# Down product of a SwiGLU layer: row tiles loaded through GpSimd's queue, and the first chunk's operands begun with the last unit's sixth product

## The chip, the cores and the metric

The kernel runs on one core of one Trainium2 chip. The metric is the device time of one execution in microseconds. Three runs of the kernel before took 2215.3 us in the median (2212.56 to 2217.59).

## What is computed

Two layers over 1024 positions of 1024 features, all in float32. Each layer is a mixer and a SwiGLU layer, each with a residual sum; the mixer of the first layer is a short gated convolution, that of the second a dilated attention. The part that matters here is SwiGLU, with 2816 hidden features:

```python
def swiglu(h, w_gate, w_up, w_down):
    return (jax.nn.silu(h @ w_gate) * (h @ w_up)) @ w_down

def reference(x, ...):
    for i in range(DEPTH):            # DEPTH = 2
        ...
        h = rms_norm(x, ffn_norm[i])
        x = x + swiglu(h, w_gate[i], w_up[i], w_down[i])
    return rms_norm(x, final_norm)
```

## The kernel before, in words

Activations lie with features on the partitions and positions along the row: `X[n]` is a tile of 128 features by 1024 positions, a "page". Half a page is 128 x 512. Pages come from a pool of 41, half pages from a pool of 20.

**Exact products from rounded parts.** TensorE is given rounded numbers, so each operand is split into a hi and a lo part: ACT copies it with rounding (hi), VectorE subtracts (lo = value - hi). A product is then three matmuls: hi hi, hi lo, lo hi. For weights this is `split` (lines 137 and 138), for activations `Strassen.hi` (lines 497 and 498).

**Strassen-Winograd.** The large products are done as products of 2 x 2 blocks with seven multiplications instead of eight, numbered m = 1 to 7 and done in the order `WINOGRAD` = 1, 2, 6, 5, 7, 3, 4. The operands of m are the sums of blocks that the method asks for. The seven share banks of PSUM: p takes m = 1, 6, 7 and 4 one on top of the other, q takes m = 2, r takes m = 5 and 3. Between two of them the bank is read (line 515 adds it to a part, line 511 copies it, line 726 adds it to x), and the next product accumulates on what is there.

**Gate and up.** `products` (line 533) runs through 22 units, the even ones gate, the odd ones up, in an order written out by hand (`unit_order`). From unit 4 on, the products m = 2 and 4 of an odd unit and of the even one before it are divided a second time (`deeper`, line 586): products (u, 11) to (u, 17), of 256 columns, written here as (21, 11) and so on. The order ends:

```python
(20,6) (20,5) (20,7) (21,1) (20,3) (21,6) (21,5) (21,7)
(21,11) (21,12) (21,15) (21,16) (21,3) (21,17) (21,13) (21,14)
```

A take of weights (line 166) also issues the splits of the weights that come one to four products later. When a block of a hidden row is done, `out` (line 1108) multiplies it by the gate (line 1114) and `store` (line 660) writes it to device memory through GpSimd's queue: rows of pairs 0 to 8 as the seven operands of the down product (`self.parts[q, m]`, lines 668 and 687), rows 18 to 21 as they are (`self.plain`, line 664).

**Down.** The down product takes the 9 pairs in three chunks of 3 (c = 0, 3, 6), each in two calls of `down` (line 720), for the output tiles 0 to 3 and 4 to 7. For each m it does two products of 9 matmuls and adds each bank to two tiles of x (line 726). Its operands come from `feed` (line 694), a generator. Each step of it loads three tiles ("hin", half pages) of the next m from `self.parts`, then splits the three tiles of the m loaded by the step before: three copies on ACT (line 497) and three subtractions on VectorE (line 498). Eight steps make one chunk: seven load, the second to the eighth split.

**What sets the order.** The schedule is manual: each engine runs its instructions in the order in which the program issues them, and waits for what an instruction needs. The function `filled` (line 756) is called after each product of the list, and there the first chunk's feed is stepped (line 770): once after each product of unit 21 from (21, 16) on, five steps. The other three steps are taken in `down(0, 0)`, one after each m. The feeds of chunks 3 and 6 are stepped in the calls of `down` before theirs.

**Queues.** All raw weights (line 151), the tiles of x (line 692), the tiles of feed (line 702) and the plain rows (line 716) are loaded through SP's queue, in the order of the program. GpSimd's queue carries the stores of `store` here.

Of the kernel before, what the change touches and what calls it, by code (L numbers as in the profile page):

```python
# [30 lines left out]
DEEP, DEEPER = (2, 4), 10  # L31
# [10 lines left out]
CONV = "conv"  # L42
# [52 lines left out]
def trunk(ctx: ExitStack, tc: tile.TileContext, x, gains_in, cwi, ck, cwo, wqkv, wo, relb,  # L95
          wg, wu, wd, oneh, ident, out):
    nc = tc.nc
# [11 lines left out]
    def half_page(name, dt=F32):  # L109
        return scope["pool"].tile([128, 512], dt, name=name, tag="half", bufs=scope["halves"])  # L110
# [47 lines left out]
    def ensure(upto):  # L158
        while op_state[0] < min(upto + 1, len(ops)):
            key = ops[op_state[0] + 1][0] if op_state[0] + 1 < len(ops) else None  # L160
            if key in sums_of:
                sums_of.pop(key)()
            made[op_state[0]] = ops[op_state[0]][1]()
            op_state[0] += 1
# [49 lines left out]
    def add_deep(unit, key, u, rows, upto):  # L214
# [27 lines left out]
        def early(op):  # L242
            w = op()
            run(*[sums_of(j, m) for j, m in enumerate(DEEP)])
            return w
# [105 lines left out]
    def run(*gens):  # L351
        for _ in zip(*gens):
            pass
        for g in gens:
            for _ in g:
                pass
# [6 lines left out]
    def both(w, ks, acts):  # L363
        banks = two_banks()
        run(product(w, ks, acts, banks))
        return banks
# [106 lines left out]
    class Strassen:  # L473
# [220 lines left out]
        def feed(self, c):  # L694

            tiles = None
            for m in WINOGRAD + (None,):
                new = None
                if m:
                    new = [half_page("hin") for k in range(self.chunk)]  # L700
                    for k in range(self.chunk):
                        nc.sync.dma_start(new[k], self.parts[c + k, m])
                if tiles:
                    lows = [self.hi(last, k, t, nc.vector)
                            for k, t in enumerate(tiles)]
                    for lo in lows:
                        lo()
                tiles, last = new, m
                if m:
                    self.b[m] = [None] * self.chunk  # L710
                    yield
# [8 lines left out]
        def down(self, c, n, feed):  # L720

            p, r = {}, {}
            later = {2: (1,), 6: (3,), 5: (4,), 7: (6,), 3: (5,), 4: (7,)}

            def add(n, h, b):
                nc.vector.tensor_tensor(out=X[n][:, half(h)], in0=X[n][:, half(h)], in1=b, op=ALU.add)  # L726

            for m in WINOGRAD:
                for k in (n, n + 2):
                    if m == 1:  # L730
                        p[k] = bank()
                    if m == 5:
                        r[k] = bank()
                    b = bank() if m == 2 else r[k] if m in (3, 5) else p[k]
                    self.mm((c, k), m, b, m in (1, 2, 5), 4)
                    add(k + (m in (5, 7, 4)), int(m in (6, 5, 7, 3)), b)
                next(feed, None)
                if c == n == 0:
                    self.load_x(*later.get(m, ()))
                    self.rest(m)  # L740
# [10 lines left out]
        def run(self, start, hooks={}):  # L751

            self.base = op_state[1]
            last = self.nu - 1

            def filled(n):
                start(n)
                if self.key != CONV:
                    self.now = n + 1
                    i = self.order.index((3, 4))  # L760
                    if n == i - 15:
                        prep.append(self.deepen(2))
                    if n == i - 5:
                        prep.append(self.deepen(4))
                    for p in prep:
                        next(p, None)
                if self.key == CONV:
                    self.below(n, last)
                else:
                    if self.order[n][0] == last and n >= self.at(last, DEEPER + 6) - self.base:  # L770
                        next(feed, None)
                    if self.order[n] == (last, DEEPER + 7):
                        self.load_x(0, 2)
                        ensure(self.at(last, DEEPER + 4) + 4)
                self.idle(n)

            prep = []
            if self.key == CONV:
                self.products(filled, hooks)
                self.first_tiles()  # L780
                return
            feed = self.feed(0)
            self.products(filled, hooks)
            for c in range(0, self.pairs, self.chunk):
                self.down(c, 0, feed)
                feed = self.feed(c + self.chunk) if c + self.chunk < self.pairs else self.feed_last()
                self.down(c, 4, feed)
            run(feed)


    class Conv(Strassen):
# [148 lines left out]
        def first_tiles(self):  # L940

            run(self.low)
            upper = self.halved(range(CO, KT))
            for n in range(KT):
                banks = two_banks()
                run(product(take(("co", 0, n), 2), range(CO), self.hid, banks))
                if n + 2 < KT:
                    self.load_x(n + 2)
                add_to_x(n, banks)
                self.step(4 if n < 2 else None)  # L950
                if n >= 3:
                    next(upper, None)
            run(upper)
            for f in range(CO):
                del self.plain[f]
# [843 lines left out]
```

## Time and profile before

| | |
|---|---|
| median of three runs | 2215.3 us |
| the profiled execution | 2215.37 us |
| its span, first to last instruction | 2213.6 us |
| TensorE clock granted, mean | 0.985 |
| ACT busy | 998.4 us, 45% |
| GpSimd busy | 147.9 us, 7% |
| DMA through SP's queue (q1), share of 16 engines | 184.80 MB, 26.2% |
| DMA through GpSimd's queue (q0) | 45.46 MB, 5.6% |
| loads of feed (line 702) | 126, of 256 KB each |
| DMA over the span | 114 GB/s |

The page gives the busy time of each engine and groups of instructions by line. The waits say which engine stood idle, in front of which line, and what ended the wait; the one named is the one that came last by the profile, which need not be the one that was needed. The timeline shows instructions in order of time: start, duration, engine, line, operation, output and input; "x3" is three of the same in a row, and brackets hold the idle time of the engine before it and what ended it. PE is TensorE, DVE VectorE, ACT ScalarE, POOL GpSimd; SPq is the queue of SP.

The two SwiGLU layers behave alike. The stretches around their down products lie at about 740 to 940 us and 1960 to 2150 us of the span.

### The profile page before, as it was taken

The numbers are of one execution on the slowest core, as the hardware profiler recorded it, in microseconds if no ns is written. First come the engines' busy times: TensorE is split into PE (matmuls) and PEld (weight loads), VectorE is DVE, ScalarE is ACT, GpSimd is POOL, SyncE is SP. The second block draws the span as 40 slices with busy tenths as digits, with TensorE's granted clock in tenths as the row PEclk, the third lists the DMA queues.
The fourth block names the chain that finished last, engine by engine and source line by source line (L and its number), as shares of the span: only waits on it lengthen the run. The fifth ranks groups of instructions, "written<-read, shape, count | busy, mean of one in ns | idle before, by whom it ended". The sixth has DMA issues, their size and how long they took to land.

```text
span 2213.6 us, 30526 instructions
## 1 busy us (share of the span) xinstructions
PE 2143.2 (97%) x11138; PEld 1829.8 (83%) x11138; DVE 1769.8 (80%) x3255; ACT 998.4 (45%) x1808; POOL 147.9 (7%) x196
## 2 busy tenths in 40 slices
PE   7899999899999999999999999999899999999998
PEld 5788887688888878878999999887678888878887
DVE  7797758888888798965677767868988888889886
ACT  6433425444444444434455555534534444444435
POOL 0000000010101000010111111110010101000000
PEclk9999999999999999999999999999999999999999
DMA  4122541222323374423333333544113323266432
GB/s 154 53 84 74 208 131 51 86 98 90 117 93 114 106 269 153 131 86 131 90 90 91 90 90 83 168 130 140 62 72 102 113 96 119 96 218 210 155 93 77
DMA packets 131263, 255.30 MB, mean 115 GB/s; under 512 B 47386, under 2 KB 58666, under 8 KB 131114
## 3 DMA queue, kind: packets, MB, share of 16 engines
q1 hardware_dynamic: 75978, 184.80, 26.2%
q0 software_dynamic: 13968, 45.46, 5.6%
q10 hardware_dynamic: 41168, 23.10, 3.6%
q8 instruction: 88, 1.44, 0.3%
q14 instruction: 61, 0.50, 0.1%
HBM read 187.04 MB, written 66.26 MB: 114 GB/s over the span
## 4 chain that ended last, share of the span: by engine, by line
PE 79%; DVE 11%; ACT 4%; DMA 3%; issue 2%; ACTq 0%; SPq 0%; DVEq 0%
PE bank L505 16%; PE bank L507 16%; PE bank L506 16%; PE bank L346 5%; PE bank L348 5%; PE bank L347 5%; PE bank L1425 4%; PE bank L600 2%; PE bank L599 2%; PE bank L597 2%; DVE b L498 2%; DVE w L138 2%; PE bank L1353 1%; PE bank L1352 1%; DVE x L438 1%
## 5 line engine op out<-in xcount | busy, mean ns | idle before, releaser
L505 PE MATMUL bank<-b,w 128*128 128x512 f32 x1784 | 706.1, 396 | 27.2 <-DVE part L515 7.3
L507 PE MATMUL bank<-b,w 128*128 128x512 f32 x1784 | 702.7, 394 | 15.8 <-DVE w L138 15.8
L506 PE MATMUL bank<-b,w 128*128 128x512 f32 x1784 | 702.7, 394 | 2.1 <-DVE b L498 2.1
L505 PEld LDWEIGHTS bank<-b,w 128*128 128x128 f32 x1784 | 339.8, 190 | 102.4 <-ACT w L137 10.5
L507 PEld LDWEIGHTS bank<-b,w 128*128 128x128 f32 x1784 | 339.4, 190 | 91.9 <-DVE w L138 20.3
L506 PEld LDWEIGHTS bank<-b,w 128*128 128x128 f32 x1784 | 340.0, 191 | 73.3 <-DVE b L498 2.9
L137 ACT ACTIVATE w<-combo 128x512 fp32r<-128x512 f32 (+2 forms) x464 | 235.0, 535 | 279.2 <-DVE combo L185 273.4
L138 DVE TENSOR_TENSOR w<-combo,w 128x512 fp32r<-128x512 f32 (+2 forms) x464 | 260.6, 575 | 69.2 <-ACT w L137 67.2
L511 ACT ACTIVATE part<-bank 128x512 f32<-128x512 f32 x168 | 99.2, 594 | 276.1 <-PE bank L507 273.6
L138 DVE TENSOR_TENSOR w<-raw,w 128x512 fp32r<-128x512 f32 (+2 forms) x316 | 168.9, 559 | 20.8 <-ACT w L137 19.1
L515 DVE TENSOR_TENSOR part<-part,bank 128x256 f32<-128x256 f32 (+1 forms) x348 | 158.6, 486 | 31.0 <-PE bank L507 15.5
L137 ACT ACTIVATE w<-raw 128x512 fp32r<-128x512 f32 (+2 forms) x316 | 150.2, 520 | 45.7 <-PE bank L507 11.3
L726 DVE TENSOR_TENSOR x<-x,bank 128x512 f32<-128x512 f32 x168 | 114.2, 680 | 30.9 <-PE bank L507 30.9
L346 PE MATMUL bank<-w_hi,w 128*128 128x512 f32 (+1 forms) x320 | 122.0, 381 | 0.0
L348 PE MATMUL bank<-w_hi,w 128*128 128x512 f32 (+1 forms) x320 | 120.0, 375 | 0.7 <-DVE w L138 0.7
L347 PE MATMUL bank<-w_lo,w 128*128 128x512 f32 (+1 forms) x320 | 119.8, 374 | 0.0
L438 DVE TENSOR_TENSOR x<-x,bank 128x512 f32<-128x512 f32 (+1 forms) x104 | 65.9, 641 | 62.6 <-PE bank L348 53.8
L185 DVE TENSOR_TENSOR combo<-raw 128x512 f32<-128x512 f32 (+1 forms) x160 | 102.9, 643 | 4.3 <-DMA raw<-in_conv_w_in 4.3
L346 PE MATMUL bank<-h_hi,w_hi 128*128 128x512 f32 x256 | 104.6, 409 | 0.7 <-ACT w_hi L137 0.7
L348 PE MATMUL bank<-h_hi,w_lo 128*128 128x512 f32 x256 | 100.2, 391 | 0.7 <-DVE w_lo L138 0.7
L347 PE MATMUL bank<-h_lo,w_hi 128*128 128x512 f32 x256 | 99.9, 390 | 0.0
L1111 ACT ACTIVATE part<-part 128x512 f32<-128x512 f32 x66 | 39.7, 628 | 110.6 <-DVE part L515 110.6
(237 smaller groups left out, 3835.2 us busy)
## 6 DMA issues: line engine op xcount, KB each, us to landing
hin<-part SPq DMA_DIRECT2D x126, 256.0 KB
raw<-in_ffn_w_gate SPq DMA_DIRECT2D x44, 512.0 KB
raw<-in_ffn_w_up SPq DMA_DIRECT2D x44, 512.0 KB
part<-sum POOLq DMA_DIRECT2D x72, 256.0 KB, 3.0
raw<-in_ffn_w_down SPq DMA_DIRECT2D x48, 384.0 KB
x<-spill SPq DMA_DIRECT2D x24, 512.0 KB
raw<-in_attn_w_qkv SPq DMA_DIRECT2D x24, 512.0 KB
raw<-in_conv_w_in SPq DMA_DIRECT2D x21, 512.0 KB
```

Source lines behind the costliest of these rows:

```text
L137: nc.scalar.activation(hi, src, AF.Copy)
L138: eng.tensor_tensor(out=lo, in0=src, in1=hi, op=ALU.subtract)
L185: eng.tensor_tensor(out=c, in0=a, in1=b, op=op)
L346: nc.tensor.matmul(b, whi[:, a], ahi[:, s], start=first, stop=False)
L347: nc.tensor.matmul(b, whi[:, a], alo[:, s], start=False, stop=False)
L348: nc.tensor.matmul(b, wlo[:, a], ahi[:, s], start=False, stop=last)
L505: nc.tensor.matmul(b, hi[:, a], bhi, start=start and k == 0, stop=False, skip_group_check=True)
L506: nc.tensor.matmul(b, hi[:, a], blo, start=False, stop=False, skip_group_check=True)
L507: nc.tensor.matmul(b, lo[:, a], bhi, start=False, stop=k == n - 1, skip_group_check=True)
L511: nc.scalar.activation(t, b, AF.Copy)
L515: nc.vector.tensor_tensor(out=t, in0=t, in1=b, op=ALU.add)
L726: nc.vector.tensor_tensor(out=X[n][:, half(h)], in0=X[n][:, half(h)], in1=b, op=ALU.add)
```

## The change

Two edits. The loads of the row tiles in `feed` go through GpSimd's queue, in all three chunks of both layers, 126 in all. And the first chunk's feed is stepped from (21, 6) on rather than from (21, 16) on, except after (21, 15) and (21, 16): after (21, 6), (21, 5), (21, 7), (21, 11), (21, 12), (21, 3), (21, 17), (21, 13) and (21, 14), nine times instead of five. The feed has eight steps, so that it is used up before `down(0, 0)`, whose own steps of it then do nothing.

```diff
@@ feed
                 if m:
                     new = [half_page("hin") for k in range(self.chunk)]
                     for k in range(self.chunk):
-                        nc.sync.dma_start(new[k], self.parts[c + k, m])
+                        nc.gpsimd.dma_start(new[k], self.parts[c + k, m])
@@ run, filled
                 else:
-                    if self.order[n][0] == last and n >= self.at(last, DEEPER + 6) - self.base:
+                    if n in feeding:
                         next(feed, None)
                     if self.order[n] == (last, DEEPER + 7):
                         self.load_x(0, 2)
@@ run
             prep = []
+
+            feeding = [n for n, um in enumerate(self.order) if n >= self.order.index((last, 6))
+                       and um not in ((last, DEEPER + 5), (last, DEEPER + 6))] if self.key != CONV else ()
             if self.key == CONV:
```

## The prediction

> **What bounds the kernel now.** I read the page first, for its span and its engines.
>
> ```profile
> span 2213.6 us, 30526 instructions
> PE 2143.2 (97%) x11138; PEld 1829.8 (83%) x11138; DVE 1769.8 (80%) x3255; ACT 998.4 (45%) x1808; POOL 147.9 (7%) x196
> ```
>
> TensorE is busy for 97% of the span, so only the time in which it waits, or runs slowly, can be won. The profiled execution took 2215.37 us, 1.8 more than its span and 0.07 more than the median of the three runs (2215.3); the sum below is made against 2215.37. Next, the waits of TensorE in the two stretches in which down products run, 740 to 940 us and 1960 to 2150 us, two rows for each:
>
> ```profile
> PE bank L505 <- ACT b L497: 3.0, 1, 3.0
> PE bank L597 <- DVE part L515: 2.0, 1, 2.0
> ...
> PE bank L505 <- ACT b L497: 3.0, 1, 3.0
> PE bank L597 <- ACT b L497: 2.0, 1, 2.0
> ```
>
> So each layer's down stage has two pauses, 5.0 us together, and no others. Where they lie is told by the timeline of TensorE (start, duration, operation, idle time before it):
>
> ```profile
> 772.68 0.28 PE L597 MATMUL bank<-b,w 128*128 128x256 f32 x1
> 776.99 0.28 PE L597 MATMUL bank<-t,w 128*128 128x256 f32 x1
> 778.43 0.40 PE L505 MATMUL bank<-b,w 128*128 128x512 f32 x1
> 783.93 0.28 PE L600 MATMUL bank<-b,w 128*128 128x256 f32 x1
> 786.21 0.36 PE L597 MATMUL bank<-t,w 128*128 128x256 f32 x1 [2.01 <-DVE part L515]
> 787.72 0.40 PE L505 MATMUL bank<-b,w 128*128 128x512 f32 x1
> 795.68 0.39 PE L507 MATMUL bank<-b,w 128*128 128x512 f32 x1
> 799.08 0.71 PE L505 MATMUL bank<-b,w 128*128 128x512 f32 x1 [3.01 <-ACT b L497]
> ...
> 1990.84 0.77 PE L505 MATMUL bank<-b,w 128*128 128x512 f32 x1 [3.02 <-ACT b L497]
> 1994.13 0.39 PE L507 MATMUL bank<-b,w 128*128 128x512 f32 x1
> ```
>
> The first pause stands before the last deep product, (21, 14). The second stands after the down product's m = 1 and m = 2, before m = 6. After it TensorE is slow for a while: in the second layer the eight matmuls from 1990.84 to 1994.13 took 3.29 us. At the pace before the pause (the 35 from 787.72 to 795.68 take 0.227 us each) eight take 1.8, so 1.5 us are lost. The 2.0 us pause has no such tail.
>
> What TensorE waits for is seen on VectorE:
>
> ```profile
> 769.12 1.43 DVE L138 TENSOR_TENSOR w<-raw,w 128x256 fp32r<-128x256 f32 x4
> 773.50 0.69 DVE L583 TENSOR_TENSOR c<-part,bank 128x512 f32<-128x512 f32 x1 [2.28 <-ACT part L511]
> 776.11 0.74 DVE L515 TENSOR_TENSOR part<-part,bank 128x256 f32<-128x256 f32 x2
> 776.77 0.68 DVE L138 TENSOR_TENSOR w<-combo,w 128x512 fp32r<-128x512 f32 x1
> 780.04 0.74 DVE L515 TENSOR_TENSOR part<-part,bank 128x256 f32<-128x256 f32 x2
> 781.38 0.69 DVE L515 TENSOR_TENSOR part<-part,bank 128x512 f32<-128x512 f32 x1 [0.59 <-PE bank L507]
> 782.71 1.89 DVE L498 TENSOR_TENSOR b<-hin,b 128x512 fp32r<-128x512 f32 x3
> 784.51 1.22 DVE L138 TENSOR_TENSOR w<-raw,w 128x256 fp32r<-128x256 f32 x3
> 785.65 0.75 DVE L515 TENSOR_TENSOR part<-part,bank 128x256 f32<-128x256 f32 x2
> 786.32 1.89 DVE L498 TENSOR_TENSOR b<-hin,b 128x512 fp32r<-128x512 f32 x3
> 791.25 1.89 DVE L498 TENSOR_TENSOR b<-hin,b 128x512 fp32r<-128x512 f32 x3
> 794.92 1.89 DVE L498 TENSOR_TENSOR b<-hin,b 128x512 fp32r<-128x512 f32 x3
> 798.25 0.68 DVE L726 TENSOR_TENSOR x<-x,bank 128x512 f32<-128x512 f32 x1
> ```
>
> In this timeline an idle time is shown in brackets. From 773.50 to 798.25 VectorE has one, of 0.59 us. The releasers follow from the code. A product accumulates into a bank (p, q or r) whose earlier content must have been read: (21, 14) waits until line 515 has read (21, 17) out of p, which starts at 785.65, and TensorE resumes at 786.21. Product m = 6 accumulates into p[k], so it waits for line 726 to add m = 1 to x: 798.25 to 798.93, and TensorE resumes at 799.08. The waits name ACT's line 497 for the second, because one of its copies happens to end near that time; but that is the hi part of m = 7, which m = 6 doesn't read. So in both pauses the bound is VectorE's queue, in its order.
>
> **The change, part by part.** *Moved: splits.* feed(0) now steps after (21, 6), (21, 5), (21, 7), (21, 11), (21, 12), (21, 3), (21, 17) and (21, 13); its ninth step finds it ended. A split of one m is three copies on ACT (line 497) and three subtractions on VectorE (line 498), 1.80 us there (782.71 to 784.51). Before, four stand ahead of the first line 726; now all seven, with 21 subtractions instead of 12.
>
> The split of m = 1 comes after (21, 5), between the weights of 769.12. These end by about 771.2, and 2.28 us of idle time follow up to 773.50: 1.80 fits, at no cost as long as its tiles are there (below); without that cover it would cost up to 1.8. The others stand after 773.50: m = 2, 6, 5, 7, 3, 4, six where there were four. VectorE has 2 x 1.80 = 3.6 us more there and gets back at most the idle 0.59, so the first line 726 moves by **+3.0 us**, and m = 6 starts 3.0 later. Down(0, 0) has less to do afterwards, but TensorE did not wait there, so nothing comes back.
>
> On the way the old pauses turn into other ones. (21, 16) needs line 515's read of 776.11, now 1.8 later: a pause of about 1.5 at 776.99. (21, 3) needs the weights of 776.77, 3.6 later: about 1. (21, 17) needs the read of 780.04, 5.4 later: about 2.5. (21, 14) still waits 2, and m = 6 some 1.5 to 2. A deep product takes 1.44 us (772.68 to 778.43 for four), so TensorE works between them. No pause is as long as the 3.0 that brought the slow matmuls; the last is nearest to the 2.0 that did not. I take the 1.5 us of slow matmuls as saved, and its other end, not saved, for the range. What is slow earlier than the last pause is absorbed in it.
>
> The Trainium skill, "TensorE: Matmul & The Clock Gate", section "Part 1: The HAM clock gate", has the clock fall after an idle window of about 3.4 us, free-running against the program. The 3.0 us pause here fell short of that figure and still brought it, in both layers. By the rule none of the new pauses would, and the end "not saved" would fall away; the row doesn't let me drop it.
>
> *Moved: the loads.* 126 loads go from SP's queue to GpSimd's. There they stand in order behind the stores of plain, which wait for VectorE, and they start by themselves, independent of TensorE.
>
> ```profile
> 766.56 9.97 SPq L702 DMA_DIRECT2D hin<-part  x6
> ...
> 754.08 1.14 POOL L664 DMA_DIRECT2D plain<-part  x2 [7.80 <-DVE part L1114]
> 775.22 0.54 POOL L664 DMA_DIRECT2D plain<-c  x1 [19.99 <-DVE c L1114]
> 783.08 0.54 POOL L664 DMA_DIRECT2D plain<-part  x1 [7.33 <-DVE part L1114]
> ...
> DMA to landing us min/median/max: 2.3/2.8/7.2
> ...
> L497 ACT ACTIVATE b<-hin x126: 612/616/634, 777.4 to 2105.6; 128x512 fp32r<-128x512 f32 x126
> ...
> plain<-part POOLq DMA_DIRECT2D x3, 256.0 KB, 6.5
> ```
>
> The tiles of m = 1 and 2 stand behind the stores of 754.08 and can go as soon as half pages are free, ten and more us before their split at about 770 and 775: free. (SP's six took 9.97 us to go out, in part, by the code, waiting for half pages; were the last of m = 2 held up until the split of m = 1, about 771, it would still land before 775.) m = 6 stands behind the store of 775.22: first load at 775.8, landed 2.8 us later (the median of GpSimd's stores of these parts; no load of this size on this queue is in the trace) at 778.6, copied by ACT in 0.62 at 779.2. VectorE would want it at 776.11 + 0.66 + 1.80 = 778.6, so it idles **0.6**. m = 3 stands behind the store of 783.08, which moves to about 788.5: first load at 789.0, landed 791.8, copied 792.4, wanted at 785.65 + 0.66 + 5.4 = 791.7: **0.7**. (The 5.4 is three more splits ahead, less the idle 0.6, plus the 0.6 of m = 6.) m = 5, 7 and 4 have no store directly ahead and at least 1 us in hand. With the shortest landing, 2.3, the two waits make 0.3; with the 6.5 of the stores in the crowded stretch, 8.7.
>
> SP's queue loses its blocks of loads. Two of the 5 us windows follow (the last two figures are the DMA share and GB/s):
>
> ```profile
> 770.00:775.00 5.00, 5.00 (x33) 4.53 (x32) 2.69 (x7) 1.83 (x6) 0.00 (x0) 1.00 0.39 108
> 780.00:785.00 5.00, 4.21 (x30) 3.77 (x29) 4.37 (x10) 3.12 (x8) 0.54 (x1) 1.00 1.07 379
> ```
>
> The raw weights and x behind these six wait up to 10 us less, and so go out while the DMA share is 0.39 rather than 1.07. That is why I take the short end for the landings. It shortens no path: VectorE never waits for raw or x here. Chunks 3 and 6 are loaded a product and more ahead of their use, without a wait of TensorE in the rows above; whatever queue they take costs nothing there, and without that cover as much as the landing is later.
>
> The Trainium skill, "DMA: Bandwidth & Descriptors", speaks against the move: its section "Specifications" gives a first byte after about 1 us from GpSimd's path and 0.6 from SP's, and "Issuing engines are not separate DMA queues" says that all queues run on the same 16 engines. By it four waits would be 0.4 us longer, an estimate of 1.6 us on top, 2222.6 in place of the sum below; no load of the trace shows it.
>
> **The sum.** For each layer + 3.0 - 1.5 + 0.6 + 0.7 = + 2.8 us; two layers + 5.6; 2215.37 + 5.6 = **2221.0 us**. All that follows in each layer is paced by TensorE and moves along.
>
> **The rivals.** *Faster.* The chain of waits can be read otherwise, that the pauses end with the tiles' landing:
>
> ```profile
> 777.73 4.98 DMA hin<-part
> ...
> 794.43 3.64 DMA hin<-part
> ```
>
> If so, earlier loads remove both pauses and the slow matmuls: 5.0 + 1.5 a layer, 13.0 in all, 2202.4. It decides if VectorE has slack between 773.50 and 798.25; the single idle time of 0.59 speaks against it. *Late tiles.* GpSimd's loads land as late as its stores did there, 6.5: + 1.5 + 8.7 a layer, 2235.8. *Nothing to measure.* The tiles are always there, and the slow matmuls are saved: + 1.5 a layer, 2218.4; if part of the 3.0 is met by idle time elsewhere, down to 2211.
>
> **How the numbers follow.** About 0.2%, 4.4 us, is what a measurement of this kernel can tell from no change; the bounds are 2210.9 and 2219.7. The forecast gets 0.52 (its own range 2219.0, with the shortest landings, to 2227, with the slow matmuls, 2 x 1.5, not saved and 3 for later landings), of which 0.10 is below 2219.7; faster 0.17; late tiles 0.11; nothing to measure 0.20. Slower 0.53, same 0.30, faster 0.17. The range 2208 to 2230 leaves out most of faster and of late tiles, some 2 in 10.
>
> **What would show it.** In each layer: VectorE without idle time, but for two, from line 583 to the first line 726, 21 subtractions of line 498 before it; line 726 about 4 us later than now; new pauses of TensorE before (21, 16), inside (21, 3) and before (21, 17); m = 6 without slow matmuls. The two, before the splits of m = 6 and m = 3, end with copies of line 497 that waited for hin. I am wrong if line 726 starts earlier than now, or if the pauses shrink in sum below 5.0 us a layer.

## The result, and the profile after

The changed kernel takes 2234.08 us (median of 5 runs, 2232.63 to 2235.58) against 2214.16 for the kernel before on the same chip (5 runs, 2212.56 to 2217.59). The ratio is 1.0088, with a 95% interval of 1.0075 to 1.0101. The prediction was 2221.0, with a range of 2208 to 2230: the sign is right, the size is not, and the time lies outside the range. The page of the changed kernel begins:

```profile
span 2232.3 us, 30560 instructions
PE 2149.5 (96%) x11138; PEld 1832.1 (82%) x11138; DVE 1772.5 (79%) x3255; ACT 999.8 (45%) x1808; POOL 216.1 (10%) x322
```

The span is 18.7 us longer. The busy time of TensorE grew by 6.3 and that of VectorE by 2.7, so most of the loss is waiting. GpSimd has 126 instructions and 68.2 us more, 0.54 us for each load that it now issues.

Where it was lost is told by two lines of code that VectorE passes once a layer: the last line 583 (the sum c of the last unit's shallow products) and the last line 726 (the end of the down stage). These are the timeline's summaries of the two, first before, then after (durations in ns, then the start of the first and of the last one in us):

```profile
L583 DVE TENSOR_TENSOR c<-part,bank x18: 679/686/689, 462.2 to 773.5; 128x512 f32<-128x512 f32 x18
L726 DVE TENSOR_TENSOR x<-x,bank x84: 671/679/689, 798.3 to 964.2; 128x512 f32<-128x512 f32 x84
L583 DVE TENSOR_TENSOR c<-part,bank x18: 679/686/690, 1653.9 to 1965.3; 128x512 f32<-128x512 f32 x18
L726 DVE TENSOR_TENSOR x<-x,bank x84: 672/679/689, 1990.0 to 2155.8; 128x512 f32<-128x512 f32 x84
```

```profile
L583 DVE TENSOR_TENSOR c<-part,bank x18: 679/686/690, 461.1 to 772.4; 128x512 f32<-128x512 f32 x18
L726 DVE TENSOR_TENSOR x<-x,bank x84: 676/681/689, 807.9 to 972.2; 128x512 f32<-128x512 f32 x84
L583 DVE TENSOR_TENSOR c<-part,bank x18: 679/686/690, 1662.7 to 1974.0; 128x512 f32<-128x512 f32 x18
L726 DVE TENSOR_TENSOR x<-x,bank x84: 673/682/689, 2009.1 to 2174.7; 128x512 f32<-128x512 f32 x84
```

I call the time from the last line 583 to the last line 726 the stage. It took 190.7 us before in the first layer (964.2 - 773.5) and 190.5 in the second; after, 199.8 and 200.7. That is 9.1 and 10.2 more, 19.3 together, all of the loss. From the first line 583 to the last, the shallow and deep products take 311.3 us in both kernels. In the stage, the first line 726 comes 35.5 us after the last line 583 where it came after 24.8: 10.7 later, in the second layer 10.4. What follows it became shorter by 1.6 us in the first layer (164.3 for 165.9) and by 0.2 in the second.

The waits of TensorE, from 740 to 980 us and from 1950 to 2180 us of the changed kernel (us in total, times, longest):

```profile
PE bank L505 <- ACT w L137: 4.4, 2, 4.0
PE bank L597 <- DVE part L515: 3.9, 3, 1.8
PE bank L505 <- DVE x L726: 2.6, 1, 2.6
...
PE bank L505 <- ACT w L137: 4.1, 1, 4.1
PE bank L597 <- DVE part L515: 4.0, 3, 1.8
PE bank L505 <- DVE x L726: 2.6, 1, 2.6
```

There are 10.9 and 10.7 us a layer where there were 5.0. The timeline of TensorE shows where, in order of time: before (21, 16), inside (21, 3), before (21, 17), before (21, 14), before m = 1, and before m = 6 in the first layer; then m = 6 in the second.

```profile
777.37 0.35 PE L597 MATMUL bank<-t,w 128*128 128x256 f32 x1 [1.33 <-DVE part L515]
783.07 0.50 PE L505 MATMUL bank<-b,w 128*128 128x512 f32 x1 [4.04 <-ACT w L137]
788.77 0.36 PE L597 MATMUL bank<-t,w 128*128 128x256 f32 x1 [0.76 <-DVE part L515]
793.71 0.36 PE L597 MATMUL bank<-t,w 128*128 128x256 f32 x1 [1.83 <-DVE part L515]
799.34 0.50 PE L505 MATMUL bank<-b,w 128*128 128x512 f32 x1 [0.34 <-ACT w L137]
808.68 0.47 PE L505 MATMUL bank<-b,w 128*128 128x512 f32 x1 [2.59 <-DVE x L726]
...
2009.90 0.77 PE L505 MATMUL bank<-b,w 128*128 128x512 f32 x1 [2.59 <-DVE x L726]
```

The longest is inside (21, 3). It waits for the hi part of its weights, which ACT copies (line 137) behind its copies of the m = 6 tiles; the lo part (line 138) stands on VectorE behind the split of the same tiles. Both engines stood still for those tiles. VectorE's timeline in the same time:

```profile
768.85 1.90 DVE L498 TENSOR_TENSOR b<-hin,b 128x512 fp32r<-128x512 f32 x3
772.40 0.69 DVE L583 TENSOR_TENSOR c<-part,bank 128x512 f32<-128x512 f32 x1 [0.31 <-ACT part L511]
773.73 1.89 DVE L498 TENSOR_TENSOR b<-hin,b 128x512 fp32r<-128x512 f32 x3
779.42 0.69 DVE L498 TENSOR_TENSOR b<-hin,b 128x512 fp32r<-128x512 f32 x1 [1.87 <-ACT b L497]
781.15 0.69 DVE L498 TENSOR_TENSOR b<-hin,b 128x512 fp32r<-128x512 f32 x1 [1.04 <-ACT b L497]
782.53 0.69 DVE L498 TENSOR_TENSOR b<-hin,b 128x512 fp32r<-128x512 f32 x1 [0.69 <-ACT b L497]
...
796.01 0.69 DVE L498 TENSOR_TENSOR b<-hin,b 128x512 fp32r<-128x512 f32 x1 [2.12 <-ACT b L497]
797.07 0.69 DVE L498 TENSOR_TENSOR b<-hin,b 128x512 fp32r<-128x512 f32 x1 [0.36 <-ACT b L497]
798.91 0.69 DVE L498 TENSOR_TENSOR b<-hin,b 128x512 fp32r<-128x512 f32 x1 [1.15 <-ACT b L497]
```

The split of m = 1 (768.85) went into the old idle time ahead of line 583, which shrank from 2.28 to 0.31. The splits of m = 6 and of m = 3 were broken up into three single subtractions, each of which waited for ACT: 3.6 us for either m, 7.2 together. ACT itself waited for the tiles, and these left GpSimd's queue just behind a store. The timeline of GpSimd:

```profile
774.11 0.55 POOL L664 DMA_DIRECT2D plain<-c  x1 [3.73 <-DVE c L1117]
774.64 4.45 POOL L702 DMA_DIRECT2D hin<-part  x8
...
790.58 0.54 POOL L664 DMA_DIRECT2D plain<-part  x1 [10.48 <-DVE part L1117]
791.11 3.23 POOL L702 DMA_DIRECT2D hin<-part  x6
```

and of ACT, whose copy of a tile starts when it has landed:

```profile
778.76 0.63 ACT L497 ACTIVATE b<-hin 128x512 fp32r<-128x512 f32 x1 [4.23 <-DMA hin<-part]
780.49 0.63 ACT L497 ACTIVATE b<-hin 128x512 fp32r<-128x512 f32 x1 [1.10 <-DMA hin<-part]
781.87 0.63 ACT L497 ACTIVATE b<-hin 128x512 fp32r<-128x512 f32 x1 [0.75 <-DMA hin<-part]
782.40 0.61 ACT L137 ACTIVATE w<-combo 128x512 fp32r<-128x512 f32 x1
...
795.35 0.63 ACT L497 ACTIVATE b<-hin 128x512 fp32r<-128x512 f32 x1 [6.33 <-DMA hin<-part]
```

The copy of 782.40 is the one that (21, 3) waits for: it ends at 783.01, and TensorE resumes at 783.07. The first m = 6 tile took 4.1 us from the start of its issue (774.64 to 778.76). The third was issued 1.1 us later and took 6.1 (about 775.75 to 781.87). The DMA engines were full in that time, as the windows of 5 us show (the last two figures are the DMA share and GB/s):

```profile
775.00:780.00 5.00, 2.70 (x21) 2.32 (x19) 3.13 (x8) 0.63 (x1) 4.41 (x9) 1.00 0.88 290
780.00:785.00 5.00, 1.85 (x5) 1.23 (x6) 3.28 (x7) 3.49 (x7) 0.10 (x1) 0.89 1.03 403
```

### The profile page after: what moved, and what is told of

It reads as the page before. It is cut to its first block, busy times and chain, and to the rows that moved or that the text cites. A ratio compares the mean times of both kernels' runs of the same rounds, so it can differ in the third digit from the quotient of the medians.

```text
span 2232.3 us, 30560 instructions
## 1 busy us (share of the span) xinstructions
PE 2149.5 (96%) x11138; PEld 1832.1 (82%) x11138; DVE 1772.5 (79%) x3255; ACT 999.8 (45%) x1808; POOL 216.1 (10%) x322
## 4 chain that ended last, share of the span: by engine, by line
PE 78%; DVE 11%; ACT 4%; issue 3%; DMA 3%; ACTq 0%; POOL 0%; SPq 0%; DVEq 0%; POOLq 0%
PE bank L505 16%; PE bank L507 16%; PE bank L506 16%; PE bank L346 5%; PE bank L348 5%; PE bank L347 4%; PE bank L1428 4%; PE bank L600 2%; PE bank L599 2%; PE bank L597 2%; DVE w L138 2%; DVE b L498 2%; PE bank L1356 1%; PE bank L1355 1%; DMA hin<-part 1%
## 5 line engine op out<-in xcount | busy, mean ns | idle before, releaser
L506 PE MATMUL bank<-b,w 128*128 128x512 f32 x1784 | 703.1, 394 | 2.4 <-DVE b L498 2.1
L506 PEld LDWEIGHTS bank<-b,w 128*128 128x128 f32 x1784 | 340.8, 191 | 74.3 <-DVE b L498 2.9
L1409 POOL PARTITION_ALL_REDUCE mb<-m x16 | 51.5, 3220 | 423.2 <-DVE m L1406 183.7
```

The lines of the kernel that those rows point to most:

```text
L506: nc.tensor.matmul(b, hi[:, a], blo, start=False, stop=False, skip_group_check=True)
```

## The experiments

Three theories were tried. **A**: two things cost, the order of VectorE's work (more splits ahead of line 726) and row tiles that come late because their loads stand behind GpSimd's stores. **B**: the path through GpSimd costs something for each of the 126 loads, wherever they stand. **C**: the early start puts too many loads on the DMA engines at once. The table has all runs. "To 726" is from the last line 583 to the first line 726 and "stage" is as above, both for the first and second layer; "idle" is VectorE's wait ahead of line 498 in the two layers, from the last weights before line 583 to past the first line 726. The ratio is to the kernel before, run on the same chip in the same turn.

| run | median us | ratio, 95% interval | to 726 | stage | idle |
|---|---|---|---|---|---|
| before | 2214.16 | 1 | 24.8, 24.7 | 190.7, 190.5 | 0, 0 |
| after | 2234.08 | 1.0088 [1.0075, 1.0101] | 35.5, 35.1 | 199.8, 200.7 | 7.2, 6.8 |
| queue only | 2231.94 | 1.0069 [1.0054, 1.0084] | 30.7, 30.1 | 198.7, 199.5 | 7.6, 8.4 |
| early start only | 2220.33 | 1.0017 [1.0007, 1.0026] | 28.7, 28.1 | 193.1, 192.6 | 0.8, 0.3 |
| one step ahead | 2219.78 | 1.0015 [1.0005, 1.0024] | 28.4, 28.7 | 192.7, 193.1 | 0.5, 0.9 |
| whole pages | 2236.57 | 1.0090 [1.0075, 1.0105] | 36.0, 37.2 | 200.4, 201.5 | 7.9, 9.1 |
| stores on SyncE | 2230.0 | 1.0061 [1.0046, 1.0076] | 30.1, 29.8 | 194.5, 194.1 | 2.2, 1.9 |
| x later | 2238.66 | 1.0100 [1.0083, 1.0117] | 37.2, 38.2 | 201.5, 202.5 | 9.0, 10.0 |
| chunks 3 and 6 only | 2217.19 | 1.0003 [0.9993, 1.0013] | 24.7, 24.7 | 190.7, 190.6 | 0, 0 |
| four ahead | 2213.07 | 0.9987 [0.9978, 0.9997] | 22.9, 23.0 | 188.7, 188.8 | 0, 0 |
| three ahead | 2206.89 | 0.9958 [0.9942, 0.9975] | 21.1, 21.2 | 186.9, 187.0 | 0, 0 |
| m = 6 behind | 2207.88 | 0.9959 [0.9945, 0.9974] | 19.3, 19.3 | 186.5, 186.5 | 0, 0 |
| three ahead, GpSimd | 2208.14 | 0.9962 [0.9948, 0.9977] | 21.2, 21.2 | 186.9, 186.9 | 0, 0 |

The stage repeats within some tenths of a us where the kernels agree in it. The medians carry another 1 to 3 us of the work between the stages, which no kernel here but one changes: from the last line 726 of the first layer to the last line 583 of the second it took 1001.1 us before, 1000.0 with three ahead and 1002.9 with three ahead on GpSimd.

**The queue alone** (the kernel before, its late start, with the loads moved):

```diff
-                        nc.sync.dma_start(new[k], self.parts[c + k, m])
+                        nc.gpsimd.dma_start(new[k], self.parts[c + k, m])
```

> The kernel before with only the queue of the row tiles changed; the feed starts late as before. Theory A (VectorE's order plus tiles that land late behind GpSimd's stores): no split moves, but the first chunk's m = 2 tiles now stand behind a store that waits for (21, 3); they land 2 to 3.5 us late in each layer: 2219 to 2222 us. Theory B (GpSimd's load path itself is the cost, 126 loads on it): the whole loss of the change, about 2232. Theory C (too many loads pulled forward onto the DMA engines): no load is pulled forward, so 2215.

It took 2231.94, so A had its size wrong and B had the price right. But the trace shows A's mechanism, larger than I had it: in VectorE's timeline of this run VectorE waits 5.6 us for the tiles of m = 2 where 2 to 3.5 were expected (three later tiles make the other 2.0 of the table),

```profile
789.09 0.69 DVE L498 TENSOR_TENSOR b<-hin,b 128x512 fp32r<-128x512 f32 x1 [4.45 <-ACT b L497]
790.58 0.69 DVE L498 TENSOR_TENSOR b<-hin,b 128x512 fp32r<-128x512 f32 x1 [0.79 <-ACT b L497]
791.63 0.69 DVE L498 TENSOR_TENSOR b<-hin,b 128x512 fp32r<-128x512 f32 x1 [0.36 <-ACT b L497]
```

and in GpSimd's they had left directly behind a store that waited for VectorE:

```profile
781.33 0.55 POOL L664 DMA_DIRECT2D plain<-part  x1 [5.71 <-DVE part L1114]
781.86 3.77 POOL L702 DMA_DIRECT2D hin<-part  x7
```

This run by itself does not tell A from B; the next ones do.

**The early start alone** (the changed kernel with the loads back on SyncE's queue):

```diff
-                        nc.gpsimd.dma_start(new[k], self.parts[c + k, m])
+                        nc.sync.dma_start(new[k], self.parts[c + k, m])
```

> The change with the row tiles on SP's queue: only the early start. Theory A: the order alone, the first line 726 about 3 us later in each layer, slow matmuls gone, tiles little late since SP waits for no store: 2217 to 2221 us, VectorE idle before line 498 under 2 us a layer. Theory B: no cost, 2215 or less. Theory C: the same loads are pulled forward, so VectorE idles as long as in the change, 7 us a layer: about 2232.

It took 2220.33, as A has it. The first line 726 is 3.9 us later than before in the first layer and 3.4 in the second; the rest of the stage is 1.5 us shorter (164.4 for 165.9). The tiles are nearly on time: VectorE's idle time ahead of line 498 is 0.8 us in the first layer and 0.3 in the second. C falls as the cause by itself: the early loads are all there, the DMA share is 1.03 and 1.04 in the two windows from 785 to 795 us, and they cost little.

**One step ahead** (the changed kernel; each step of the first chunk's feed issues the loads of the step after it, into whole pages):

```diff
-            for m in WINOGRAD + (None,):
+            for i, m in enumerate(ms + [None]):
...
+                if m and m not in ready:
+                    load(m)
+                if c == 0 and i + 1 < len(ms):
+                    load(ms[i + 1])
```

> The change, but the first chunk's tiles are loaded one step earlier, still through GpSimd's queue, into whole pages so that no half page is waited for: the m = 6 tiles stand ahead of the store they stood behind. Theory A: VectorE's idle time before line 498 falls from 7.2 us a layer to under 2, and what is left is the order: 2217 to 2222 us. Theory B: the same number of loads on the same queue, about 2232. Theory C: as many loads pulled forward and earlier, about 2232.

With the same queue and the same number of loads it took 2219.78, only 3.4 us more than the kernel before in the same turn (2216.37). The two stages are 4.6 us longer than before where those of the changed kernel are 19.3 longer, and they are those of the early start alone. B falls. VectorE's waits from 764 to 810 us, in the changed kernel and in this one:

```profile
DVE b L498 <- ACT b L497: 7.2, 6, 2.1
```

```profile
DVE b L498 <- ACT b L497: 0.5, 2, 0.3
```

The loads of this run also land quicker: the 16 that GpSimd issued from 765 to 800 us have a median of 4.2 us to landing, the 17 of the changed kernel 6.2. But they leave so much earlier that 6.2 would have been enough: the m = 6 tiles are issued from 765.96 on, ahead of the store, and their split begins at 778.21. GpSimd's timeline of this run:

```profile
765.96 1.91 POOL L703 DMA_DIRECT2D hin<-part  x3 [0.81 <-PE bank L507]
774.84 0.54 POOL L664 DMA_DIRECT2D plain<-c  x1 [6.97 <-DVE c L1124]
```

**Whole pages** is the control for it, since two things had changed:

```diff
-                    new = [half_page("hin") for k in range(self.chunk)]
+                    new = [half_page("hin") if c else page("hin")[:, :HALF] for k in range(self.chunk)]
```

> The changed kernel with the first chunk's row tiles in whole pages instead of halves, but not loaded a step ahead: the control for the run that loads one step ahead, which changed both. Theory A (the loads stand behind the store in GpSimd's queue, and the step that issues them is the step that uses them): as the changed kernel, 2231 to 2236, VectorE idle before line 498 some 7 us a layer. Rival (the wait for a free half page on GpSimd's queue made the tiles late): as the run one step ahead, about 2220, with VectorE idle under 2 us.

2236.57, 0.6 above what A expected, with 7.9 and 9.1 us of idle time: free space for the tiles brings nothing, only the earlier issue does. That it is more than 7.2 lies at m = 3, whose split waits 4.8 us instead of 3.6; the x rows leave at 791.27 here, as they do in the run "x later" below.

**The stores on SyncE's queue** (the changed kernel; the feed-forward's stores of its down parts):

```diff
-                nc.gpsimd.dma_start(self.plain[2 * q + c[0]][:, half(c[1])], g)
+                (nc.gpsimd if self.key == CONV else nc.sync).dma_start(self.plain[2 * q + c[0]][:, half(c[1])], g)
```

> The changed kernel with the stores of the feed-forward's down parts (line 664) issued by SyncE, so that no store stands ahead of the row tiles on GpSimd's queue; the number of loads there and the early start stay. Theory A: VectorE's idle time before line 498 falls from 7.2 to under 2 us a layer and the time to 2217 to 2223; SyncE's raw and x tiles now stand behind these stores, and if they come late instead, waits for them take the place and are shown as such. Theory B (the loads on GpSimd's path cost, wherever they stand): as the changed kernel, 2231 to 2235. Theory C (too many loads at once): 2225 or above, since nothing less is loaded in the stage.

The median, 2230.0, misses what A expected, 2217 to 2223, and the trace says why. In the stage A is right: without a store ahead of the loads, VectorE's idle time falls from 7.2 to 2.2 us and the stage from 199.8 to 194.5. The m = 3 tiles are on time; those of m = 6 are still 2.2 late: two of the three left GpSimd's queue only after it had waited 2.00 and 1.18 us for VectorE, by the code for a free half page. Of the 11.9 us that the two stages win, 7.5 are lost before them, in the stretch from the first line 583 to the last: it takes 314.5 and 315.6 us instead of 311.3. SyncE's queue now has the same fault, its raw weights stand behind a store, and VectorE waits for them:

```profile
743.92 0.33 SPq L664 DMA_DIRECT2D plain<-part  x1
744.35 0.41 SPq L151 DMA_DIRECT2D raw<-in_ffn_w_gate  x1
```

```profile
748.38 0.69 DVE L185 TENSOR_TENSOR combo<-raw 128x512 f32<-128x512 f32 x1 [3.82 <-DMA raw<-in_ffn_w_gate]
```

**Chunks 3 and 6 only** (the kernel before; the first chunk's loads stay with SyncE):

```diff
-                        nc.sync.dma_start(new[k], self.parts[c + k, m])
+                        (nc.gpsimd if c else nc.sync).dma_start(new[k], self.parts[c + k, m])
```

> The kernel before with the row tiles of chunks 3 and 6 alone on GpSimd's queue; the first chunk's stay on SyncE's and begin as late as before. Theory A (the tiles of the first chunk stand behind GpSimd's stores, and nothing else costs): these 84 of the 126 loads have no store ahead of them and over 5 us before their use, so 2214 to 2219, no difference from before. Theory B (each load costs something on GpSimd's path): 84 of the 126 loads of the run with the queue alone, which lost 15.6 us, so about 10.4 us, 2226 to 2228. PE's waits from 830 to 935 us: none by A.

The ratio is 1.0003, its interval reaches from 0.9993 to 1.0013: 84 loads on GpSimd's queue cost nothing that this can tell, and the stages are those of before (190.7 and 190.6).

**x later** (the changed kernel; were the landings long because x was loaded in the same time?):

```diff
+                    if self.order[n] == (last, DEEPER + 4):
+                        self.load_x(0, 2)
                     if self.order[n] == (last, DEEPER + 7):
-                        self.load_x(0, 2)
                         ensure(self.at(last, DEEPER + 4) + 4)
```

> The changed kernel with SyncE's loads of the x rows 0 and 2 begun after the last unit's last product instead of its fourth from last, so that they aren't on the DMA engines while the m=6 tiles land. If those loads are what stretched the landings: the m=6 tiles land in about 3 us, VectorE's idle time before line 498 falls from 7.2 to 5 or 6 us a layer, and the time to 2229 to 2232. If the row tiles crowd each other (eight loads in one go): no change, 2232 to 2235. If x comes late: a wait before the first line 726, and above 2235.

2238.66, which none of the three expected: it is above 2235, but there is no wait for x. The idle time of the m = 6 split stayed at 3.5 us (1.81, 1.22 and 0.49), and the window from 780 to 785 us is as full without x (403 GB/s): so x alone was not what stretched those landings. In the changed kernel the first m = 6 tile had landed, at 778.76, before x was issued, at 779.06. The two x rows now go out at 790.79, just ahead of the m = 3 tiles at 791.43, and the split of m = 3 waits 5.4 us (4.26, 0.52 and 0.67) instead of 3.6. One megabyte more on the engines at that moment cost 1.8 us of lateness, and 3.2 in the second layer; at the 403 GB/s of the full windows it takes 2.6.

**Three ahead**. The order term of A can also be turned round: if each split ahead of line 726 costs, fewer should pay. This is the kernel before, loads on SyncE's queue, with four feed steps: one early, so that its split falls into VectorE's idle time before line 583, and the rest later.

```diff
-                    if self.order[n][0] == last and n >= self.at(last, DEEPER + 6) - self.base:
+                    if self.order[n][0] == last and self.order[n][1] in (6, 5, DEEPER + 7, DEEPER + 4):
```

> The kernel before with four feed steps among the products instead of five, after (21, 6), (21, 5), (21, 17) and (21, 14): the split of m = 1 falls into VectorE's idle time before line 583, m = 5 moves behind the first line 726, all on SP's queue. Theory A: two splits instead of four stand between line 583 and the first line 726, which comes 3.6 us earlier, and the slow matmuls go: about 5 us a layer, 2205 us. The rival reading, that the pauses end when the tiles land or are copied: no gain, 2213 to 2218, since three of the four later operands are begun no earlier.

2206.89, ratio 0.9958: faster than both kernels. Two splits, 3.6 us, have gone from between line 583 and line 726, and the first line 726 comes 3.7 us earlier in the first layer (21.1 for 24.8), 3.5 in the second. TensorE's two pauses of 2.0 and 3.0 us are now, from 740 to 980 us:

```profile
PE bank L505 <- ACT b L497: 2.1, 3, 1.2
PE bank L597 <- DVE part L515: 0.2, 1, 0.2
```

The stages are 3.8 and 3.5 us shorter, not the 5 that A expected. The slow matmuls are gone, but the first row holds three pauses: 1.22 us before m = 6, then 0.39 and 0.52 us further on, where there were none. So what follows the first line 726 takes 165.8 us, as before. The other 2 us of the difference of medians lie between the stages.

**Four ahead** puts one split back: `in (6, 5, DEEPER + 7, DEEPER + 3, DEEPER + 4)`.

> The kernel before, SyncE's queue, with five feed steps between the last unit's products where the run that reached 2207 had four, so one split more on VectorE ahead of line 726. Theory A (each split that stands between line 583 and the first line 726 costs its 1.8 us, once a layer, as long as none is taken away that its own product then waits for): 2207 + 2 x 1.8 = 2210.5, between 2209 and 2212. Rival (that run gained by the pauses that it avoided alone): below 2209.

The stage gives A's price to the tenth, 188.7 for 186.9, 1.8 a layer. The median, 2213.07, is 1.1 us above the end of what was expected. In the same turn the last run below, whose stage is 186.9 too, took 2208.14: of the 4.9 us between them 3.6 are the stage's, the rest lies outside it.

**m = 6 behind** takes one more away: `in (6, 5, DEEPER + 4)`.

> The kernel before with only four feed steps (three early and one late) left between the last unit's products, where the run that reached 2207 had four in other places: the split of the m=6 tiles moves behind the first down products. By A each split fewer before line 726 brings that line about 1.8 us earlier, but the split of m=6 then lies just ahead of its own matmuls, so no further gain: 2206, give or take 2. Rival (fewer splits ahead always pays, whatever follows): about 2203.

2207.88, as A has it (the expectation speaks of four feed steps; the edit leaves three). The first line 726 is 1.8 us earlier still (19.3), but the stage gains 0.4 only: TensorE now waits for the split of m = 6 itself, `PE bank L506 <- DVE b L498`, 1.1 us a layer, and for nothing earlier. So fewer splits pay until the next product waits for its own.

**Three ahead on GpSimd's queue** joins the order of three ahead with the loads one step ahead of the run above.

> The order of the run that reached 2207 (four feed steps between the last unit's products), but with all row tiles on GpSimd's queue as in the changed kernel, the first chunk's loaded one step ahead into whole pages. Theory A: the queue costs nothing where its loads are issued a step early, and gains nothing either, since no row tile was late on SyncE's queue there: 2205 to 2209. If the queue itself has a price (theory B): above 2212. If taking the tiles off SyncE's queue is worth something by itself (raw and x earlier): below 2204.

2208.14, with the stage of three ahead, 186.9 in both layers. The queue costs nothing in this place if the loads are issued a step early, and it brings nothing.

## Why the prediction was right in sign and wrong in size

- **The order of VectorE's work, + 3.0 us a layer: right.** With the early start alone the first line 726 moved by 3.9 and 3.4, of which 0.8 and 0.3 are VectorE's idle time for tiles: 3.1 in either layer. Two splits more are 3.6, and the idle 0.59 that I had taken off is no longer in VectorE's timeline. In the changed kernel it moved by 10.7 and 10.4, which without the 7.2 and 6.8 of idle time is about 3.5; the 0.4 more is about what the broken splits cost, six single subtractions of 0.69 us where three in a row take 1.89.
- **The split of m = 1 at no cost: right.** It went into the idle time ahead of line 583.
- **The slow matmuls saved, - 1.5: right once, wrong once.** After line 726 the stage is 1.5 us shorter with the early start alone, and 1.6 in the first layer of the changed kernel. In its second layer the pause of 2.59 us ahead of m = 6 brought the slow matmuls back (0.77 us for the first one, at 2009.90), and 0.2 is left of the gain. I had taken that pause for 1.5 to 2 us.
- **Chunks 3 and 6 at no cost: right**, by the run that moves them alone.
- **Which loads come late: right.** It was those of m = 6 and m = 3, behind the two stores that I named, and VectorE waited for no others.
- **How late, + 0.6 and + 0.7: this is the step that failed**, the landing time in the sum: "landed 2.8 us later (the median of GpSimd's stores of these parts; no load of this size on this queue is in the trace)". The rest of the step holds. VectorE was ready for m = 6 at 777.55 (779.42 - 1.87), the first load began at 774.64, and with 2.8 and a copy of 0.62 the wait would have been 0.5. It was 1.87 because the first tile took 4.1. Even in the quiet stretch of chunks 3 and 6 such a load took 3.5 (below), so that the median of the stores was too short for a load there too. A second error lies beside it: I followed one tile, and a split needs three. They are issued about 0.55 us apart, which a subtraction of 0.69 would have covered, but landed at 778.76, 780.49 and 781.87, so that the second and third add 1.04 and 0.69. For m = 3 it is the same, 2.12, 0.36 and 1.15. Together 7.2 us a layer, not 1.3.
- **"That is why I take the short end for the landings": wrong.** I took the DMA share of 0.39 in the old trace for that of the new. But what is freed on SyncE's queue does not vanish, it goes out earlier; and the store that held the m = 6 tiles back held back those of m = 5 and m = 7 too, so eight loads left in one go. The share became 0.88 and 1.03 just when the tiles of m = 6 were on their way.
- **The pauses.** (21, 16) was put at 1.5 and took 1.33; (21, 14) at 2, 1.83; inside (21, 3), at 1, it took 4.04, the lateness of the m = 6 tiles, which came by way of ACT's copy of the weights and not of VectorE's line 138, as I had it; (21, 17), at 2.5, then had only 0.76 left to wait. "No pause is as long as the 3.0" failed with the 4.04: from 783.88 to 787.40 eight matmuls took 0.44 us each. They cost nothing of their own, since the waits for VectorE behind them took them in, as the prediction had it for what is slow before the last pause.

The rival "late tiles", 2235.8 with a chance of 0.11, is what happened, by its mechanism and nearly its size. It was held for unlikely by the choice of the short landing, and both ends, 2.3 and 6.5, stood in the prediction: the 6.5 came from stores in a crowded stretch, and the new loads were in one. That the size fits so well is in part luck: the 6.5 was meant for the first tile of a split, and the first took 4.1 and 4.2; the rest came from the second and third. Theory A's sum with the measured terms, the 3.1 of the early start alone among them, is + 3.1 - 1.5 + 7.2 = 8.8 in the first layer, for 9.1 measured, and + 3.1 - 0.2 + 6.8 = 9.7 in the second, for 10.2; the broken splits are most of the rest.

The Trainium skill, "DMA: Bandwidth & Descriptors", section "Specifications", with its 0.4 us more for a first byte through GpSimd, gave an estimate of 1.6 us on top. No run here can tell such a price: three ahead has the same stage by either queue, but by GpSimd's its loads leave a step early, which would hide it. The same page's section "Issuing engines are not separate DMA queues", by which the DMAs of all engines run on the same 16 engines, agrees with the crowded windows: there the loads of both queues together moved 403 GB/s at a DMA share of 1.03.

What stays open is how the 4 to 6 us of a landing divide. That a crowd adds to them is shown for m = 3 by the run with x later. For m = 6 that run only shows that x alone is not the reason; that its eight tiles and the raw weights crowd each other was argued from the windows and not tried. Nor did any run separate GpSimd's path from the crowd in these landings: the runs show what the loads cost when they come late, not why a landing there takes 4 to 6 us.

## What to carry to other kernels

A load moved to another engine's queue inherits whatever stands ahead of it there: name the last store before it and the instruction that this waits for, and issue the load a step before it is wanted, which here took back 14.7 of the 19.3 us that the two stages had lost, with whole pages for the first chunk's tiles. Time a group of loads by its last one, with the landing of the stretch as the change will make it, and not as it was. And where the vector engine paces a stage, count what stands in its queue ahead of the one operation that the matmuls wait for: two splits of 1.8 us fewer there made the stage 3.5 to 3.8 us shorter, until the next product had to wait for its own split.

## What the runs showed of the hardware

A load of 256 KB on GpSimd's queue took a median of 3.5 us to land in the quiet stretch of chunks 3 and 6 (830 to 935 us, 30 loads, DMA share 0.30 to 0.51), and 6.2 in the stretch from 765 to 800 us (17 loads, DMA share up to 1.03). Both are of the changed kernel.

Where the matmuls are slow, the granted clock is about half: 0.53 from 1990.80 to 1994.00 us before, 0.50 from 2009.50 to 2012.50 in the changed kernel. The length of a pause alone did not decide whether the matmuls after it were slow. 3.01 us were followed by slow ones before (0.71 us for the first, in the prediction's rows), and 2.59 us in the second layer of the changed kernel but not in the first. With four ahead, 3.02 us were not, in either layer (granted clock 1.00 in the 4 us behind each):

```profile
797.03 0.47 PE L505 MATMUL bank<-b,w 128*128 128x512 f32 x1 [3.02 <-ACT b L497]
...
1987.99 0.47 PE L505 MATMUL bank<-b,w 128*128 128x512 f32 x1 [3.02 <-ACT b L497]
```

The Trainium skill, "TensorE: Matmul & The Clock Gate", section "Part 1: The HAM clock gate", has the clock fall after at least one idle window of about 3.4 us, and the windows run free of the program. These rows don't agree with 3.4 us of idle time as a floor, since 3.01 was enough, and 2.59 once. Windows that run free would explain why the same pause falls either way; no run here shifts a pause against them, so that this stays open.
